# Token mixers as stepped generators between the halves of large weight products

## The chip, the cores and the metric

The kernel runs on one core of a Trainium2 chip: TensorE (PE) multiplies matrices into the eight banks of PSUM, VectorE (DVE), ScalarE (ACT) and GpSimd (POOL) do the elementwise work, and SyncE (SP) issues all the transfers of this kernel in one queue. Each engine takes its instructions in the order in which the program lists them. The metric is device time of one execution in microseconds (us), median of several runs.

## The reference

Two layers of a decoder trunk run over 280 columns: 16 meta tokens, 256 prompt tokens and one token of each of 8 samples. Per layer:

```
proj = x @ w_in                       # 16,400 columns: Mamba-2, HGRN2, retention, gates
y_m = mamba_branch(z, xbc, dt, ...)   # conv, silu, SSD recurrence, 4 groups of 4 heads
y_h = hgrn_branch(q, f, i, g, ...)    # gated linear recurrence, 8 heads of 128 x 128
y_r = retention_branch(q, k, v, g, ..)# 4 heads, keys 256, values 512, rotary
mixed = g_m*(y_m @ w_br_m) + g_h*(y_h @ w_br_h) + g_r*(y_r @ w_br_r)
x = LN1(alpha*x + mixed @ w_out)
x = LN2(alpha*x + SwiGLU(x))          # width 2816
```

The prompt runs through each recurrence in chunk form (scores of token pairs, weighted by decays, times values); each sample updates a stored state by one token. All new states are outputs. Everything is float32.

## The kernel before, in words

The stream stands transposed: a tile is 128 channels by 280 tokens. A **block** is 128 output columns of a weight matrix: `wblock` loads it into `raw`, ACT copies its high part to `wh`, DVE subtracts to get the rest in `wl`, and `project` (called by `in_block` and `br_block`) makes 24 **large products** of it on PE into a `pp` bank, three for each of 8 slices of the contraction. Layer 1 skips the 16 meta columns where nobody reads them, so many of its products have 264 columns.

The **mixers** are the three recurrences. They are many **small products** (128x128 transposes, products with 16 to 512 columns, many of them only 32 output columns wide) with elementwise work between them, in `mx`, `vb` and `po` banks.

- `hgrn_mix` handles a pair of heads. It builds eight levels of decayed operands (`level`: POOL subtracts the reference from the upper half and the lower half of each block, ACT takes the exponential, DVE multiplies by q and k, or POOL where the half length is 64 or more), and `diag` multiplies each level, 18 products of 32 or 24 columns. Masked sums (`pr`, `pt`, `scz`) then go into the output products. `hgrn_samples` updates eight samples' states.
- `mamba_group` and `mamba_samples` do the same for a group of four SSD heads; `ret_mix` and `ret_samples` for a retention head. `ret_samples` is already a generator: `tick`, called after each block, runs one step of it.
- `behind` makes the first of a group of small products wait for the last of all their operands.

In program order a whole stage of blocks stands first and the mixers that its predecessor fed come after it: stage p is `hgrn_proj(p + 1)`, six blocks, and four blocks of gates, then `hgrn_mix(p)`, `hgrn_samples(p)`, `mamba(p + 1)`. A scheduler at build time orders each engine's instructions by program order among those it holds to be ready, so small products fall between large ones where it expects a large one to wait. Weight splits get ahead by `boost` places of the program order (`BOOST`).

The stages that the text speaks of, per layer, with the blocks that bound them: A, B and C (10 blocks each: the projections of head pairs 1, 2 and 3 with their gates), D (8 blocks, retention head 0), E (8 blocks, retention head 1), then the tail (retention heads 2 and 3, the Mamba branch product, the three merge gates and the HGRN branch product; 56 blocks).

Of the kernel before, what the change touches and what calls it, by code (L numbers as in the profile page):

```python
# [8 lines left out]
F32 = mybir.dt.float32  # L9
# [6 lines left out]
P = 128  # L16
# [4 lines left out]
BUFS = {"px": 8, "py": 22, "pa": 10, "pm": 9, "tt": 3, "tm": 4, "ps": 2, "pb": 1, "vh": 4}  # L21
# [3 lines left out]
BOOST = (0, 10, 60)  # L25

RATE = 1
# [59 lines left out]
def body(ctx: ExitStack, tc: tile.TileContext, a: dict):  # L87
# [65 lines left out]

    def mm(out, lhsT, rhs, start, stop):
        return TE.matmul(out, lhsT, rhs, start=start, stop=stop, skip_group_check=True)  # L155
# [39 lines left out]
    def project(ps, w, rhs_hi, rhs_lo, nk, first=True, last=True):  # L195
        late[0] -= 1
        n = 1 if late[0] < 0 else nk
        for k0 in range(0, nk, n):
            for part in range(2):
                for k in range(k0, min(k0 + n, nk)):  # L200
                    hi, lo = (x[:, k, :] for x in w)
                    if part == 0:
                        mm(ps, hi, rhs_hi(k), first and k == 0, False)
                        mm(ps, lo, rhs_hi(k), False, False)
                    else:
                        mm(ps, hi, rhs_lo(k), False, last and k == nk - 1)
# [9 lines left out]
    later = []  # L216
    credit = [0.0]

    def tick(n=RATE):
        credit[0] = credit[0] + n if later else 0.0  # L220
        while later and credit[0] >= 1:
            credit[0] -= 1
            if next(later[0], 0) == 0:
                later.pop(0)
# [253 lines left out]
    flip = [0]  # L478

    def diag_of(parts):  # L480

        t = qd[flip[0] % 2]
        flip[0] += 1
# [48 lines left out]
    def ret_mix(l, h, proj):  # L532
# [21 lines left out]
        sub(end[64:96, 256:272], sc[0:32, 416:432], f32(end[0:32, 256:272]))  # L554

        vhl = flat("vh", dt=F32R)
        vt = []
        for t0, n in TOK:
            ps = mxt()
            for j in range(4):  # L560
                TE.transpose(ps[:n, 128 * j:128 * j + 128], blk(vch, j)[:, t0:t0 + n], ident)
# [4 lines left out]
            else:  # L566
# [3 lines left out]
                vt.append((hi, lo))  # L570
        kt = [pair("pm", 256, F32R), pair("pm", 256, F32R)]
        for tb, (t0, n) in enumerate(TOK):
            ps = mxt()
            for i in range(2):
                TE.transpose(ps[:n, 128 * i:128 * i + 128], k[:, i, t0:t0 + n], ident)
            kd = kdc[:n, tb, h:h + 1]
            hi, lo = (end[0:32, 0:256], end[64:96, 0:256]) if n < P else (kt[0][:, tb, :], kt[1][:, tb, :])
            V.tensor_scalar(hi, ps[:n, 0:256], kd, None, ALU.mult)
            stt(lo, ps[:n, 0:256], kd, f32(hi), ALU.mult, ALU.subtract)
        V.tensor_copy(end[32:64, 0:256], f32(end[0:32, 0:256]))  # L580

        y = pairs("py", 2)
        for j in range(4):
# [8 lines left out]
            copy(blk(y, j)[:, 0:TP], ps[:, 0:TP])  # L592

        def final(after=None):
            for i in range(2):
                so = flat("pm")
                ps = mxt()
                ks = slice(128 * i, 128 * i + 128)
                for tb in range(2):
                    (vh, vl), (kh, kl) = vt[tb], (x[:, tb, ks] for x in kt)  # L600
                    ins = mm(ps, kh, vh, tb == 0, False)
                    if after is not None and tb == 0:
                        nosync(raw(ins), raw(after))
                    mm(ps, kh, vl, False, False)
                    mm(ps, kl, vh, False, False)
                mm(ps, end[0:96, ks], vhl[0:96, :], False, True)
                copy(so, ps)
                store(out=a["ret_p"][l, h, i], in_=so)

        if h < 3:  # L610
            final()
        return y, vhl, columns(q, k), final

    def ret_norm(y):
        sq = pairs("pm", 2)
        for j in range(2):
            S.activation(sq[j][:, :, 0:TP], y[j][:, :, 0:TP], AF.Square)
        add(sq[0][:, :, 0:TP], sq[0][:, :, 0:TP], sq[1][:, :, 0:TP])
        add(sq[0][:, 0, 0:TP], sq[0][:, 0, 0:TP], sq[0][:, 1, 0:TP])
        st = mxt()  # L620
# [6 lines left out]
    def ret_samples(l, h, y, vhl, qk):  # L627
        gam = 1.0 - 2.0 ** (-5.0 - h)
        t = diag_of([qk[:, i, :] for i in range(2)])
        acc = po.tile([P, 512], F32, tag="po", name="po")  # L630
# [21 lines left out]
        os_ = flat("ps")  # L652
        copy(os_[:, 0:256], acc[:, 0:256])
# [132 lines left out]
    def mamba_tok(dd):  # L786
# [3 lines left out]
        for tb, (t0, m) in enumerate(TOK):  # L790
            TE.transpose(ps[:m, 128 * tb:128 * tb + 128], tk[:, t0:t0 + m], ident)
# [9 lines left out]
    def mamba_group(l, g, tok, dab, x, bc):  # L801
        Bc, Cc = blk(bc, g), blk(bc, 4 + g)
        btok = flat("pm", 384).rearrange("p (j t) -> p j t", j=3)
        xd = [pair("pm", 256), pair("pm", 256)]
        xdt = [xd[0][:, 0, :], xd[0][:, 1, :], xd[1][:, 0, :]]
        xt = [pair("pm", 256), pair("pm", 256)]
        xtl = [xt[0][:, 0, :], xt[0][:, 1, :], xt[1][:, 0, :]]
# [6 lines left out]
        copy(cb[0:32, 0:16], ps[0:32, 0:16])  # L814
        ps = mxt()
        for tb, (t0, n) in enumerate(TOK):
            TE.transpose(ps[:n, 128 * tb:128 * tb + 128], Bc[:, t0:t0 + n], ident)
        copy(btok[:, 0:2, :], ps[:, 0:256].rearrange("p (j t) -> p j t", j=2))
        S.activation(btok[0:32, 2, :], ps[0:32, 256:384], AF.Copy, scale=tmask[0:32, :])
        for tb, (t0, n) in enumerate(TOK):  # L820
            ps = mxt()
            for i in range(2):
                TE.transpose(ps[:n, 128 * i:128 * i + 128], x[g][:, i, t0:t0 + n], ident)
            mul(xdt[tb][:n, :].rearrange("p (h q) -> p h q", q=64), ps[:n, 0:256].rearrange("p (h q) -> p h q", q=64),
                tok[:n, tb, 4 * g:4 * g + 4].unsqueeze(2).to_broadcast([n, 4, 64]))
            mul(xtl[tb][:n, :].rearrange("p (h q) -> p h q", q=64), xdt[tb][:n, :].rearrange("p (h q) -> p h q", q=64),
                tok[:n, tb, 64 + 4 * g:64 + 4 * g + 4].unsqueeze(2).to_broadcast([n, 4, 64]))
        rows = dr.tile([NS, 256], F32, tag="rows", name="rows")
        store(out=rows, in_=xdt[2][24:32, :])

        ps = mxt()
        for tb, (t0, n) in enumerate(TOK):
            mm(ps[:, 0:256], btok[:n, tb, :], xtl[tb][:n, :], tb == 0, tb == 2)
        so = flat("pm", 256)
        copy(so, ps[:, 0:256])
        store(out=a["ssm_p"][l, g], in_=so)
        for i in range(2):
            b = 2 * g + i
            es = []
            for hh in range(2):  # L840
                h = 2 * b + hh
                pe = mxt()
                mm(pe[:, :SW], selh[:, h:h + 1].to_broadcast([P, P]), r32(cumhl), True, False)
                mm(pe[:, :MW], identb, negb, False, True)
                e = flat("pm", SW)
                act(e[:, 160:SW], pe[:, 160:SW], AF.Exp, bias=tok[:, 0, 32 + h:33 + h])
                act(e[:, 16:160], pe[:, 16:160], AF.Exp, bias=tok[:, 1, 32 + h:33 + h])
                act(e[0:32, 0:16], pe[0:32, 0:16], AF.Exp, bias=tok[0:32, 2, 32 + h:33 + h])
                mul(e[:, 16:SW], e[:, 16:SW], cb[:, 16:SW])
                up = mul(e[0:32, 0:16], e[0:32, 0:16], cb[0:32, 0:16])  # L850
                es.append(e)

            py = mxt()
            for tb, (t0, n, c0, c1) in enumerate(((0, P, 160, SW), (128, P, 16, 160), (256, 32, 0, 16))):
                for hh, e in enumerate(es):
                    hs = slice(64 * (2 * i + hh), 64 * (2 * i + hh) + 64)
                    ins = mm(py[64 * hh:64 * hh + 64, t0:TP], xdt[tb][:n, hs], e[:n, c0:c1], tb == 0, tb == 2)
                    if tb == hh == 0:
                        behind(ins, up)
            yv = x[g][:, i, 0:TP]  # L860
            stt(yv, yv, pcol(("dskip", l), b), py[:, 0:TP], ALU.mult, ALU.add)
        return rows

    def mamba_samples(l, g, dab, vhl, x, bc):
        Bc, Cc = blk(bc, g), blk(bc, 4 + g)
        t = diag_of([Cc[:, TP:T]])
        acc = po.tile([P, 512], F32, tag="po", name="po")
        for c in range(2):
            st = state(a["s_ssm"][l, g, c], "p (b q) -> p b q", b=4)
            s4 = st.rearrange("p b (h q) -> p b h q", q=64)  # L870
            mul(s4, s4, dab[:, 4 * c:4 * c + 4, 4 * g:4 * g + 4].unsqueeze(3).to_broadcast([P, 4, 4, 64]), G)
            for bb in range(2):
                vb = everywhere(vhl, 2 * c + bb)
                for b2 in range(2):
                    b = 4 * c + 2 * bb + b2
                    up = stt(st[:, b % 4, :], vb[:, 256 * b2:256 * b2 + 256], Bc[:, TP + b:TP + b + 1],
                             st[:, b % 4, :], ALU.mult, ALU.add)
# [568 lines left out]
```

## Time and profile before

| | us |
|---|---|
| median of 3 runs | 1934.88 (1929.5 to 1938.77) |
| the profiled execution, its own time | 1943.87 |
| its span, first to last instruction | 1941.8 |
| PE busy in the span | 1855.2 (96%) |
| DVE busy | 1360.4 (70%) |
| ACT busy | 1066.7 (55%) |
| POOL busy | 467.6 (24%) |
| mean granted clock of TensorE | 0.978 of full |

The profile is of one execution, 9 us above the median of the plain runs. Matmuls are pipelined, so a busy PE can still be a PE at half its clock or one that changes its tile shape between products.

### The profile page before, as it was taken

Reading aid. Unit: us, or ns where it says so; the run is one execution under the profiler, and the core shown is the slowest. Engines: PE = TensorE matmul, PEld = TensorE weight load, DVE = VectorE, ACT = ScalarE, POOL = GpSimd, SP = SyncE. Lnnn points to the kernel's source line nnn. Section 1 sums busy time; section 2 is a strip of 40 time slices with the busy share of each in tenths; the row PEclk is TensorE's granted clock in tenths of the full one; section 3 lists DMA queues with packets and bytes.
Section 4 is the critical chain, followed back from the end, with each engine's and each line's share of the span. In section 5 each row is a group of like instructions: output and inputs, shape, how many; then the busy total and the mean of one; then the engine's idle time right before and its main releaser. Section 6 shows DMA issues by size and latency. Waiting matters only on the chain.

```text
span 1941.8 us, 39091 instructions
## 1 busy us (share of the span) xinstructions
PE 1855.2 (96%) x15746; PEld 1718.3 (88%) x15746; DVE 1360.4 (70%) x2129; ACT 1066.7 (55%) x1826; POOL 467.6 (24%) x526
## 2 busy tenths in 40 slices
PE   8989999999999999999999999999999999999997
PEld 7978787888888999999989787878888889989997
DVE  7787877867656675655468899987767557666654
ACT  6666655545554544544356776755556546454443
POOL 2025535511011023000120255544110010230002
PEclk9989998999999999999999999999999999999999
DMA  5544564557678555455545446655766875545553
GB/s 198 182 152 170 191 211 162 200 209 256 224 283 299 196 174 165 140 174 173 164 137 173 163 165 204 209 201 184 249 231 248 293 263 182 184 144 183 181 176 102
DMA packets 115125, 378.44 MB, mean 195 GB/s; under 512 B 13120, under 2 KB 18688, under 8 KB 114944
## 3 DMA queue, kind: packets, MB, share of 16 engines
q1 hardware_dynamic: 114944, 375.94, 57.5%
q8 instruction: 124, 2.03, 0.4%
q14 instruction: 57, 0.47, 0.1%
HBM read 317.61 MB, written 58.28 MB: 194 GB/s over the span
## 4 chain that ended last, share of the span: by engine, by line
PE 77%; DVE 10%; DMA 5%; ACT 4%; issue 2%; POOL 1%; SPq 0%; DVEq 0%; ACTq 0%; POOLq 0%
PE pp L155 63%; PE mx L155 9%; DVE pm L140 3%; PE po L155 3%; DMA st<-s_ret 2%; DVE wl L140 2%; PE vb L155 1%; DVE pa L140 1%; ACT wh L137 1%; DMA ret_s<-st 1%; DVE py L140 1%; DVE st L152 1%; POOL hpt L140 1%; ACT pm L137 1%; POOL pm L140 1%
## 5 line engine op out<-in xcount | busy, mean ns | idle before, releaser
L155 PE MATMUL pp<-px,wh 128*128 128x280 f32 (+1 forms) x5504 | 1100.9, 295 | 17.9 <-DVE px L285 7.8
L155 PEld LDWEIGHTS pp<-px,wh 128*128 128x128 f32 x5504 | 889.4, 192 | 32.5 <-issue 13.5
L140 DVE TENSOR_TENSOR wl<-raw,wh 128x1024 fp32r<-128x1024 f32 (+1 forms) x472 | 608.6, 1292 | 307.2 <-ACT wh L137 302.9
L155 PE MATMUL pp<-px,wl 128*128 128x280 f32 (+1 forms) x2752 | 808.1, 294 | 0.5 <-DVE wl L140 0.5
L137 ACT ACTIVATE wh<-raw 128x1024 fp32r<-128x1024 f32 (+1 forms) x472 | 493.9, 1048 | 330.6 <-PE pp L155 207.0
L155 PEld LDWEIGHTS pp<-px,wl 128*128 128x128 f32 x2752 | 528.1, 192 | 6.2 <-issue 2.9
L155 PE MATMUL pp<-py,wh 128*128 128x280 f32 (+1 forms) x1984 | 381.6, 289 | 1.2 <-ACT py L137 0.8
L155 PEld LDWEIGHTS pp<-py,wh 128*128 128x128 f32 x1984 | 313.6, 188 | 3.9 <-issue 1.6
L155 PE MATMUL pp<-py,wl 128*128 128x280 f32 (+1 forms) x992 | 285.9, 288 | 1.5 <-DVE wl L140 1.5
L155 PEld LDWEIGHTS pp<-py,wl 128*128 128x128 f32 x992 | 186.7, 188 | 2.9 <-DVE wl L140 2.0
L155 PE MATMUL mx<-pm 128*32 128x16 f32 (+11 forms) x1968 | 144.8, 238 | 22.9 <-DVE pm L140 16.6
L155 PEld LDWEIGHTS mx<-pm 128*32 128x32 f32 (+4 forms) x1968 | 107.0, 136 | 55.4 <-issue 15.4
L140 POOL TENSOR_TENSOR pa<-pa 128x280 f32<-128x280 f32 (+3 forms) x56 | 76.8, 1381 | 310.3 <-DVE pa L140 249.7
L140 POOL TENSOR_TENSOR pm<-pm 128x272 f32<-128x272 f32 (+2 forms) x104 | 106.1, 1050 | 109.3 <-ACT pm L137 92.2
L152 DVE SCALAR_TENSOR_TENSOR st<-vb,qks,st 128x512 f32<-128x512 f32 x128 | 90.6, 745 | 53.0 <-PE vb L155 21.4
L140 DVE TENSOR_TENSOR pa<-pa,pp 128x280 f32<-128x280 f32 (+1 forms) x152 | 66.2, 435 | 47.2 <-PE pp L155 35.0
L130 ACT ACTIVATE pa<-pp 128x280 f32<-128x280 f32 (+1 forms) x124 | 48.4, 391 | 92.2 <-PE pp L155 92.2
L643 ACT ACTIVATE st<-st 128x1024 f32<-128x1024 f32 x64 | 67.7, 1057 | 56.3 <-DMA st<-s_ret 39.1
L140 POOL TENSOR_TENSOR pa<-px 128x560 f32<-128x560 f32 (+1 forms) x16 | 25.4, 1589 | 275.2 <-DVE py L140 275.0
L155 PE MATMUL po<-st,qd 128*32 128x256 f32 (+1 forms) x896 | 71.6, 369 | 1.7 <-DVE st L152 1.7
L137 ACT ACTIVATE pa<-pp 128x280 f32<-128x280 f32 (+1 forms) x80 | 31.7, 396 | 71.1 <-PE pp L155 70.8
L137 ACT ACTIVATE pm<-mx 128x256 f32<-128x256 f32 (+5 forms) x120 | 47.6, 412 | 40.9 <-PE mx L155 29.0
(233 smaller groups left out, 1800.2 us busy)
## 6 DMA issues: line engine op xcount, KB each, us to landing
raw<-w_in SPq DMA_DIRECT2D x256, 512.0 KB, 3.4
raw<-w_ffn_in SPq DMA_DIRECT2D x88, 512.0 KB, 3.2
st<-s_ret SPq DMA_DIRECT2D x64, 512.0 KB, 5.2
ret_s<-st SPq DMA_DIRECT2D x64, 512.0 KB, 3.7
vh<-rows SPq DMA_DIRECT2D x64, 256.0 KB, 4.6
raw<-w_br_r SPq DMA_DIRECT2D x32, 512.0 KB, 3.3
raw<-w_ffn_out SPq DMA_DIRECT2D x32, 512.0 KB, 3.9
st<-s_ssm SPq DMA_DIRECT2D x16, 512.0 KB, 4.8
```

Of the source, the lines that this page charges most:

```text
L130: ins = S.activation(out, in_, func, **kw)
L137: return S.activation(out, in_, AF.Copy)
L140: return e.tensor_tensor(out, x, y, op)
L152: return V.scalar_tensor_tensor(out, x, s, y, op0, op1)
L155: return TE.matmul(out, lhsT, rhs, start=start, stop=stop, skip_group_check=True)
L643: S.activation(st, st, AF.Copy, scale=gam)
```

## The change

`hgrn_mix`, `hgrn_samples` and `hgrn_final` become one generator, `hgrn`; the Mamba functions become `mamba`; `ret_mix` becomes a generator too. A step between two `yield`s holds one group of small products and the elementwise work of operands that a later step multiplies. `begin` puts a generator into `plan` with the number of its steps and of the half blocks they are spread over, and `tick` now runs after each half of a block (after slice 3 of 8 and at its end) and advances every generator in `plan` by its share. `put` ties each small product behind the last large product that the program has listed, without a semaphore. The mixers of pair p now run during the blocks of pair p + 1, one stage sooner for HGRN; `finish` runs what is left of them at the end of a stage.

Level subtraction becomes one DVE instruction over the whole block, an absolute value on ACT, and an exponential of the negative. `behind` goes. Turned tails (the transposed last 32 tokens) go to half of one fixed bank (`ends`), sample sums to its other half (`sums`), so the `mx` bank of the tails' scores is free again. Weight splits of the mixers' and later stages get ahead by 100 places. `pm` has 12 buffers in place of 9, and smaller tiles get 7 of their own (`pq`).

```diff
-BUFS = {"px": 8, "py": 22, "pa": 10, "pm": 9, "tt": 3, "tm": 4, "ps": 2, "pb": 1, "vh": 4}
+BUFS = {"px": 8, "py": 22, "pa": 10, "pm": 12, "pq": 7, "tt": 3, "tm": 4, "ps": 2, "pb": 1, "vh": 4}
-BOOST = (0, 10, 60)
-RATE = 1
+BOOST = (0, 100, 100)
+NM, NH, NR, NSR = 16, 17, 15, 12
...
+    place = [None]
+    def large(out, lhsT, rhs, start, stop):
+        place[0] = raw(TE.matmul(out, lhsT, rhs, start=start, stop=stop, skip_group_check=True))
+    def put(ins):
+        if place[0] is not None:
+            nosync(raw(ins), place[0])
+        return ins
...
+            if n == 1 and k0 == nk // 2 - 1:
+                tick()
...
+    plan = []
+    def begin(gen, steps, halves, credit=0.0):
+        plan.append([gen, steps / halves, credit])
+        return plan[-1]
+    def tick():
+        for s in list(plan):
+            s[1:] = s[1], s[2] + s[1]
+            while s[2] >= 1:
+                s[2] -= 1
+                if next(s[0], 0) == 0:
+                    plan.remove(s)
+                    break
...
+    both = po.tile([P, 512], F32, tag="po", name="po")
+    sums, ends = both[:, 0:256], both[:, 256:512]
...
-                sub(eu, cu, ref, G)
-                sub(el, ref, cl, G)
-                act(e[:, :, 0:n], e[:, :, 0:n], AF.Exp)
+                c4, e4 = (x[:, :, 0:n].rearrange("p i (b h) -> p i b h", h=2 * h) for x in (cum, e))
+                sub(e4, c4, c4[:, :, :, h - 1:h].to_broadcast([P, 2, nb, 2 * h]))
+                S.activation(e[:, :, 0:n], e[:, :, 0:n], AF.Abs)
+                act(e[:, :, 0:n], e[:, :, 0:n], AF.Exp, scale=-1.0)
...
+        e1 = level(1)
+        yield 1
+        diag(0, k, q)
+        yield 1
...
+        diag(1, k, e0)
+        e3 = level(3)
+        yield 1
+        diag(2, e1, e1)
+        e4 = level(4)
+        yield 1
...
-        hp = [hgrn_gate(l, 0, tiles)]
...
+        for p in range(4):
+            begin(hgrn(l, p, hp, hg, oh), NH, 19)
+            begin(mamba(l, p, td, dd, xm, bc, z, ym), NM + 2 * (p == 0), 19)
             if p < 3:
-                hp.append(hgrn_proj(l, p + 1))
-                z.append(smooth_pair(l, "py", True))
-                hg.append(smooth_pair(l, "py", False))
+                hp = hgrn_proj(l, p + 1)
+                z, hg = smooth_pair(l, "py", True), smooth_pair(l, "py", False)
+                finish()
...
-            smp = hgrn_mix(l, p, hp[p])
-            hgrn_samples(l, p, *smp)
...
-                mamba(p + 1)
...
+        rps = [rp]
+        begin(retention(), 4 * NR, 64)
...
+                    begin(samples(), 4 * NSR, 112)
...
-    nc = _bacc.Bacc("TRN2", target_bir_lowering=False, num_devices=1, dynamic_dma_scratch_size=8192)
+    nc = _bacc.Bacc("TRN2", target_bir_lowering=False, num_devices=1, dynamic_dma_scratch_size=2048)
```

## Rows read from the trace of the kernel before

**Rows 1.** The page's busy times by engine, and TensorE's granted clock in 40 slices.

```profile
PE 1855.2 (96%) x15746; PEld 1718.3 (88%) x15746; DVE 1360.4 (70%) x2129; ACT 1066.7 (55%) x1826; POOL 467.6 (24%) x526
...
PEclk9989998999999999999999999999999999999999
```

**Rows 2.** Busy time by stretch, layer 0: stages A to E, then the tail.

```profile
core 0: us, PE busy (x) PEld busy (x) DVE busy (x) ACT busy (x) POOL busy (x), PEclk, DMA share, GB/s
106.40:160.00 53.60, 47.59 (x395) 41.73 (x394) 43.56 (x71) 30.98 (x68) 25.98 (x19) 0.90 0.52 171
160.00:223.30 63.30, 59.64 (x637) 51.09 (x634) 50.73 (x97) 40.77 (x94) 26.10 (x29) 0.95 0.54 188
223.30:287.60 64.30, 59.86 (x637) 51.17 (x634) 50.55 (x98) 40.82 (x94) 29.58 (x33) 0.95 0.57 194
287.60:348.20 60.60, 54.24 (x587) 45.88 (x585) 46.35 (x100) 33.43 (x79) 33.51 (x37) 0.92 0.51 175
348.20:394.10 45.90, 42.36 (x457) 38.24 (x454) 34.88 (x65) 25.40 (x50) 21.92 (x31) 0.96 0.55 187
394.10:648.40 254.30, 250.20 (x1919) 222.25 (x1917) 162.83 (x231) 135.17 (x209) 29.01 (x28) 1.00 0.74 255
```

**Rows 3.** The same view, layer 1: stages A to E, then the tail.

```profile
1079.60:1129.70 50.10, 45.33 (x396) 39.93 (x394) 45.94 (x69) 32.62 (x70) 22.81 (x16) 0.93 0.50 170
1129.70:1191.30 61.60, 57.12 (x635) 49.26 (x633) 55.11 (x103) 43.49 (x98) 27.12 (x33) 0.97 0.55 189
1191.30:1253.00 61.70, 57.28 (x637) 49.16 (x635) 55.67 (x103) 43.14 (x98) 37.29 (x36) 0.97 0.58 200
1253.00:1311.60 58.60, 53.10 (x589) 44.79 (x586) 49.97 (x103) 34.26 (x81) 32.34 (x37) 0.94 0.58 198
1311.60:1357.60 46.00, 42.78 (x455) 39.21 (x454) 35.60 (x65) 25.21 (x50) 22.76 (x32) 0.93 0.57 188
1357.60:1606.50 248.90, 244.41 (x1920) 215.61 (x1918) 163.83 (x231) 134.63 (x209) 26.98 (x29) 1.00 0.73 255
```

**Rows 4.** Timeline, TensorE, stage B, layer 0: start, length; pp are large products.

```profile
164.96 0.42 PE L155 MATMUL pp<-px,wh 128*128 128x280 f32 x2
...
165.35 0.42 PE L155 MATMUL pp<-px,wh 128*128 128x280 f32 x2
...
166.78 0.42 PE L155 MATMUL pp<-px,wh 128*128 128x280 f32 x2
167.12 0.52 PE L155 MATMUL mx<-pm 128*32 128x16 f32 x36
167.57 0.40 PE L155 MATMUL pp<-px,wl 128*128 128x280 f32 x1
...
172.61 2.96 PE L155 MATMUL mx<-pm 128*128 128x128 f32 x24
176.63 0.80 PE L155 MATMUL mx<-pm 128*128 128x128 f32 x2 [1.05 <-POOL pm L140]
...
181.05 0.67 PE L155 MATMUL pp<-px,wh 128*128 128x280 f32 x2
...
181.75 0.67 PE L155 MATMUL pp<-px,wh 128*128 128x280 f32 x2
```

**Rows 5.** TensorE's longest waits in stages A to E of layer 1.

```profile
engine line waited for: us in total, times, longest us
PE mx L155 <- DVE pm L140: 9.1, 9, 2.4
PE mx L972 <- ACT pm L137: 9.0, 3, 3.8
```

**Rows 6.** DVE by groups, stage B, layer 1: count, busy, mean ns, idle before.

```profile
L140 DVE TENSOR_TENSOR pm<-pm,pa 128x544 f32<-128x544 f32 x1 | 0.7, 726 | 0.4 <-ACT pm L130 0.4
```

**Rows 7.** Groups of POOL's instructions in stage B of layer 1.

```profile
L140 POOL TENSOR_TENSOR pm<-pm 128x256 f32<-128x256 f32 x6 | 6.5, 1108 | 4.5 <-PE mx L155 4.5
L140 POOL TENSOR_TENSOR pm<-pm 128x272 f32<-128x272 f32 x5 | 6.3, 1275 | 0.0
```

**Rows 8.** Groups of ACT's instructions in stage B of layer 1.

```profile
L130 ACT ACTIVATE pm<-pm 128x544 f32<-128x544 f32 x3 | 1.8, 640 | 0.0
```

More of the change, by code (lines that the diff above doesn't have):

```diff
@@ L213, in body, with finish @@
     lead = 0
[L216 to L224, printed above, removed]
+    plan = []
[10 more added lines that the diff above has]
+                    break
+    def finish(*some):
+        some = list(some or plan)
+        while some:
+            for s in list(some):
+                if s not in plan or next(s[0], 0) == 0:
+                    some.remove(s)
+                    if s in plan:
+                        plan.remove(s)
     def in_block(l, c0=0):
@@ L592, in ret_mix @@
             copy(blk(y, j)[:, 0:TP], ps[:, 0:TP])
[L594 to L617, printed above, removed]
+            if j % 2:
+                sq.append(pair("pm"))
+                S.activation(sq[-1][:, :, 0:TP], y[j // 2][:, :, 0:TP], AF.Square)
+            yield 1
         add(sq[0][:, :, 0:TP], sq[0][:, :, 0:TP], sq[1][:, :, 0:TP])
         add(sq[0][:, 0, 0:TP], sq[0][:, 0, 0:TP], sq[0][:, 1, 0:TP])
+        yield 1
+        for i in range(2):
+            if h < 3:
+                final(i)
+            yield 1
         st = mxt()
@@ L628, in ret_samples @@
         gam = 1.0 - 2.0 ** (-5.0 - h)
-        t = diag_of([qk[:, i, :] for i in range(2)])
-        acc = po.tile([P, 512], F32, tag="po", name="po")
+        t = diag_of([qk[:, i, :] for i in range(2)], h % 2)
+        acc = sums
         def products(b):
@@ L814, in mamba_group, with weighted @@
         copy(cb[0:32, 0:16], ps[0:32, 0:16])
+        yield 1
+        def weighted(out, v, w, n):
+            mul(out.rearrange("p (h q) -> p h q", q=64), v.rearrange("p (h q) -> p h q", q=64),
+                w.unsqueeze(2).to_broadcast([n, 4, 64]))
+        xd, xt = pair("pm", 256), pair("pm", 256)
+        xde, xte = flat("pq", 256), flat("pq", 256)
+        ps = sums
+        for i in range(2):
+            turn(ps[:32, 128 * i:128 * i + 128], x[g][:, i, TAIL:T])
+        weighted(xde[:32], ps[:32, 0:256], tok[:32, 2, heads], 32)
@@ new lines, in mamba @@
+        weighted(xte[:32], xde[:32], tok[:32, 2, 64 + 4 * g:68 + 4 * g], 32)
+        rows = dr.tile([NS, 256], F32, tag="rows", name="rows")
+        store(out=rows, in_=xde[24:32, :])
+        yield 1
+        ps = mxt()
+        for tb in range(2):
+            for i in range(2):
+                turn(ps[:, 256 * tb + 128 * i:256 * tb + 128 * i + 128], x[g][:, i, 128 * tb:128 * tb + 128])
+        for tb in range(2):
+            weighted(xd[:, tb, :], ps[:, 256 * tb:256 * tb + 256], tok[:, tb, heads], P)
+            weighted(xt[:, tb, :], xd[:, tb, :], tok[:, tb, 64 + 4 * g:68 + 4 * g], P)
@@ L815, in mamba_group @@
+        yield 1
+        btok, be = flat("pq", 256), flat("pq", P)
         ps = mxt()
         for tb, (t0, n) in enumerate(TOK):
[L817 to L827, printed above, removed]
@@ L831, in mamba_group @@
+        scores(4 * g)
+        yield 1
         ps = mxt()
-        for tb, (t0, n) in enumerate(TOK):
-            mm(ps[:, 0:256], btok[:n, tb, :], xtl[tb][:n, :], tb == 0, tb == 2)
-        so = flat("pm", 256)
+        for tb in range(2):
+            mm(ps[:, 0:256], btok[:, 128 * tb:128 * tb + 128], xt[:, tb, :], tb == 0, False)
+        mm(ps[:, 0:256], be[:32], xte[:32], False, True)
+        so = flat("pq", 256)
         copy(so, ps[:, 0:256])
         store(out=a["ssm_p"][l, g], in_=so)
[L837 to L868, printed above, removed]
+        yield 1
+        scores(4 * g + 1)
+        yield 1
+        t = diag_of([Cc[:, TP:T]], 0)
+        acc = sums
+        def states(c):
             st = state(a["s_ssm"][l, g, c], "p (b q) -> p b q", b=4)
             s4 = st.rearrange("p b (h q) -> p b h q", q=64)
-            mul(s4, s4, dab[:, 4 * c:4 * c + 4, 4 * g:4 * g + 4].unsqueeze(3).to_broadcast([P, 4, 4, 64]), G)
+            mul(s4, s4, dab[:, 4 * c:4 * c + 4, heads].unsqueeze(3).to_broadcast([P, 4, 4, 64]), G)
@@ L886, in mamba_samples @@
+        scores(4 * g + 2)
+        yield 1
+        outputs(0)
+        yield 1
+        scores(4 * g + 3)
+        yield 1
+        read(st, 0)
+        st = states(1)
+        yield 1
+        outputs(1)
+        yield 1
+        read(st, 1)
+        os_ = flat("ps", 256)
+        copy(os_, acc)
+        yield 1
         for i in range(2):
-            mm(ps[:, 8 * i:8 * i + 8], os_[:, 128 * i:128 * i + 128], sumsel, True, True)
+            mm(acc[:, 8 * i:8 * i + 8], os_[:, 128 * i:128 * i + 128], sumsel, True, True)
@@ L904, in mamba_final @@
             stt(t[:, i, c], t[:, i, c], pcol(("mnw", l), 2 * g + i), rs, ALU.mult, ALU.mult)
-        return split(t)
+        ym.append(split(t))
     def hgrn_blocks(l, tiles):
@@ L1037, in hgrn_mix @@
         mul(kt[:, :, 0:TP], kt[:, :, 0:TP], k[:, :, 0:TP])
-        E = [level(LEVELS[x], 256) for x in range(4, 8)]
+        yield 1
+        diag(4, e3, e3)
         late_q = wk.tile([P, 2, 16], F32, tag="hlq", bufs=2, name="hlq")
@@ L1264, in body @@
         res.norm(("ln1_g", l), ("ln1_b", l))
-        smp[3](res.last)
+        for i in range(2):
+            final(i, res.last)
         hid = ([], [])
```

377 lines of the change are left out of this document (215 added, 162 removed).

## The prediction

> **What bounds the kernel now.** I read the page first: PE is busy nearly throughout, and its granted clock is below full in a few slices only [rows 1]. Since a share over the whole span hides the stages, I then asked for the busy times of the stages in which the mixers run. PE stands idle there for the length less its busy time: in A to E 6.0 + 3.7 + 4.4 + 6.4 + 3.5 = 24.0 us in layer 0 [rows 2] and 4.8 + 4.5 + 4.4 + 5.5 + 3.2 = 22.4 us in layer 1 [rows 3]; in the tails 4.1 and 4.5 us. The granted clock is 0.90 to 0.97 in A to E and 1.00 in the tails. [...] All that PE could gain is then 55.0 us of waits and 32.3 us of clock, 87 us.
>
> The timeline shows where both come from. Large products follow each other by 0.13 us (three in 0.39 us [rows 4]). Then a run of 24 small ones starts at 172.61, a wait for POOL of 1.05 us follows, and no large product stands between; afterwards three large ones take 0.70 us in place of 0.39, half the clock. The waits of A to E are for DVE's and ACT's results, up to 3.8 us at once [rows 5].
>
> The second thing to see is DVE. In stages B and C of layer 1 it works 55.1 to 55.7 of 61.6 us [rows 3], in layer 0 50.7 of 63.3 [rows 2]. PE at full clock and without waits would need 57.1 - 1.8 = 55.3 us in layer 1's B. Two engines have the same floor there.
>
> **The change part by part.** *Large and small products*: their numbers stay. Counting the breaks in PE's timeline gives 79 visits to small products in A to E of each layer, one per half block already, and some 140 in a whole layer. After it I count from the steps some 145. A visit costs little of its own: 36 products of 16 columns between two large ones delay the second by 167.57 - 166.91 - 0.13 = 0.53 us, nearly all their own 0.52 [rows 4]. I cost the new visits at nothing; if each of 20 more per pair cost half a visit, that is a rival below.
>
> *Spreading*: a stretch like 172.61 to 178 cannot come up where each half block, 12 large products and some 1.5 us, has one step of each generator behind it. I expect the clock to stay up in A to E, and PE's floors to be what it is busy now less the clock's share: in layer 0 A 42.2, B 56.5, C 56.6, D 49.4, E 40.5 us [rows 2], in layer 1 41.8, 55.3, 55.4, 49.6, 39.6 [rows 3].
>
> *HGRN one stage sooner*: it leaves E and enters A. Its work on PE is B less A, 14.3 and 13.5 us; on DVE 50.7 - 43.6 = 7.2 and 55.1 - 45.9 = 9.2. So A becomes a stage like B, and E needs 26.2 and 26.1 us of PE, 27.7 and 26.4 of DVE. In sum nothing, but the retention steps begin on a freer E.
>
> *Level subtraction*: six per pair go from two POOL instructions each to one on DVE. DVE takes 6 x 0.70 us (a two-input instruction of 544 elements takes 0.726 us, 512 elements are 6% less) = 4.2 us a pair [rows 6]. POOL loses some 13 us a pair [rows 7]. Instructions of DVE and POOL that run side by side slow each other, by how much in sum no row says: nothing given back is one bound, all 4.2 us the other; I take half, so DVE gains 2 us of work a pair. ACT takes six more of 0.62 to 0.64 us [rows 8], at most 3.8 us a pair; it is busy 43.5 of 61.6 us [rows 3] and this hides in its 18 us. Without that cover it would cost 8 x 3.8 = 30 us.
>
> *Queues*: POOL's multiplications of states and of the coarse levels come sooner, with 13 us of subtraction gone ahead of them. SP gets the mixers' loads, broadcasts and stores between the weight loads of the same stage, one stage earlier for HGRN; a store that waits for its data holds the next weight load behind it. The transfers fill 0.50 to 0.58 of the engines in A to E [rows 2, 3], and three raw and four split buffers stand ahead of PE, over 20 us at 6 us a block. I take nothing. *Banks, buffers, dropped semaphores, scratch*: a bank less is held over the levels; sums and tails share a bank and may wait for each other. Nothing either way, inside the allowance below. *Splits 100 places ahead*: no work, but mixer instructions on DVE stand behind them; also in the allowance.
>
> *The sum.* Each stage takes its larger floor and an allowance for waits. Today B of layer 0 stands 6.8 us above its floor and B of layer 1 6.3; with operands made steps ahead I allow 2.5 us (E, nearly empty, 1.5). Layer 0: A, B, C 59.0 each, D 51.9, E 29.2: 258.1 against 287.7, -29.6. Layer 1, where DVE's floor is the larger one (57.1, 57.1, 57.7, 52.0, 26.4): 59.6 + 59.6 + 60.2 + 54.5 + 27.9 = 261.8 against 278.0, -16.2. The tails have 8.6 us of waits; their steps were spread before, so I take 2. Together -48 us. The profiled execution, 1943.87, becomes 1896; the median of the plain runs stands 9 us lower, and 1934.9 - 48 = 1887.
>
> **The rivals.** *A wait at each visit (slower).* PE is in order: a small product that waits holds the second half of its block too. Visits number some 290 in both layers and today's waits 55 us, 0.19 us each. With all the clock regained the change loses once a visit waits 87 / 290 = 0.30 us; at 0.40 us it costs 116 - 87 = 29 us more: 1964. For it: DVE already at 0.9 in layer 1, given more work and the splits in front of the mixers', single waits of up to 3.8 us. Against: those waits come now from operands asked for at once, and the new steps make them one or more half blocks, 3 us, ahead.
>
> *DVE, or tile shapes, eat the gain (no change).* If POOL gives nothing back and each stage stays as far above its floor as now, 6.5 us, eight stages lose 4 us each and layer 1 another 2 each: 48 - 32 - 8 leaves -8 us, 1927. The other road to the same place is more openings of narrow tile shapes: 20 more visits a pair, the two generators' groups apart, at half of 0.53 us are 5.3 us a pair, 42 us for eight: 1929. Against the second: the groups themselves stay whole, and by the steps as written a pair has 56 changes of tile shape where I count 57 now. [...]
>
> *The order on PE stays as it was (no change).* The scheduler places instructions by what it holds ready, and small products stood between large ones before. Then 8 x 2 us on DVE count at most in layer 1's four pairs: 1935 to 1943.
>
> *All of it (faster still).* No allowance (-23 us), the tails' waits gone (-6.6), POOL giving back all (-6): 1851.
>
> **How the numbers follow.** About 0.5%, 10 us, is what a measurement of this kernel can tell from no change. The forecast case, 1870 to 1905, gets 0.46; a weaker one, with an allowance between 2.5 and 6 us, 1905 to 1925, gets 0.14; below 1870 0.13; no change 0.13; the waits 0.14. So faster 0.73, same 0.13, slower 0.14. The range runs from the full gain, 1852, to 1942, where the slower case begins; the forecast's own is 1870 to 1905.
>
> **What would show it.** Right: granted clock of 0.99 or more in A to D; A as long as B and C, 58 to 61 us; E at 28 to 32; PE's idle time in A to E at half or less of 46 us; POOL's busy time down by about 100 us and DVE's up by no more than 20. Wrong: large products that wait for wl, or small ones for DVE, at most visits; DVE busy for a whole stage with PE idle by 5 us; the clock still falling inside A to E, which would mean that steps bunch up as before.

## The result and the profile after

The kernel after the change takes 1910.39 us (median of 4 runs, 1903.8 to 1915.73), the kernel before 1934.73 beside it: a ratio of 0.9874 [0.9835, 0.9913], 24.3 us less. The forecast was 48 us less, 1887 us, in a range of 1870 to 1905. The profiled execution went from 1943.87 to 1915.73 us, 28.1 us less, and the stages below are compared in these two.

The page of the kernel after, busy times and granted clock, answers to [rows 1]:

```profile
PE 1838.5 (96%) x15746; PEld 1710.0 (89%) x15746; DVE 1351.5 (71%) x2177; ACT 1078.4 (56%) x1838; POOL 392.5 (21%) x430
...
PEclk9998999999999999999999989999999999999999
```

POOL lost 75.1 us. DVE, which took over 48 level subtractions, did not gain but lost 8.9 us. The stages answer to [rows 2, 3]: A to E and the tail of layer 0, then of layer 1:

```profile
core 0: us, PE busy (x) PEld busy (x) DVE busy (x) ACT busy (x) POOL busy (x), PEclk, DMA share, GB/s
105.80:176.60 70.80, 61.47 (x641) 52.30 (x639) 59.61 (x124) 47.50 (x107) 28.36 (x24) 0.93 0.51 171
176.60:238.20 61.60, 57.29 (x636) 49.33 (x634) 53.89 (x106) 43.41 (x97) 22.76 (x22) 0.99 0.63 208
238.20:300.20 62.00, 58.11 (x635) 50.34 (x634) 52.44 (x105) 43.29 (x97) 20.32 (x21) 0.97 0.59 201
300.20:348.00 47.80, 47.80 (x559) 41.17 (x557) 41.43 (x93) 32.21 (x72) 15.95 (x20) 0.98 0.59 191
348.00:387.60 39.60, 39.33 (x298) 36.83 (x295) 27.58 (x49) 22.80 (x40) 8.54 (x10) 1.00 0.50 168
387.60:626.10 238.50, 236.90 (x1860) 213.78 (x1859) 155.15 (x212) 125.17 (x188) 30.01 (x27) 1.00 0.76 270
1057.50:1128.60 71.10, 60.40 (x635) 51.17 (x634) 60.69 (x120) 47.27 (x105) 26.45 (x23) 0.90 0.47 155
1128.60:1189.20 60.60, 57.87 (x636) 49.47 (x635) 55.16 (x110) 45.07 (x101) 20.57 (x22) 0.97 0.57 196
1189.20:1248.40 59.20, 56.46 (x636) 49.09 (x635) 55.36 (x109) 44.36 (x99) 20.02 (x23) 0.97 0.61 211
1248.40:1300.40 52.00, 49.53 (x566) 42.03 (x564) 47.11 (x95) 34.28 (x76) 22.74 (x24) 0.97 0.62 210
1300.40:1340.20 39.80, 38.79 (x299) 36.31 (x296) 27.78 (x50) 22.80 (x40) 8.01 (x11) 1.00 0.51 174
1340.20:1576.00 235.80, 232.12 (x1860) 207.12 (x1859) 154.34 (x212) 124.95 (x188) 30.25 (x28) 1.00 0.76 265
```

HGRN's products did move: A has some 640 products where it had 395, E 298 where it had 457. From A to the tail's end layer 0 takes 520.3 us in place of 542.0, layer 1 518.5 in place of 526.9, together 30.1 us less; 2 us of it are lost elsewhere. Of the 30.1, PE's idle time (length less busy) gives 12.3: it was 55.0 with the tails, and is now 17.8 + 19.6 in A to E and 5.3 in the tails, 42.7. The other 17.8 are PE's busy time; the mean clocks account, as an estimate, for up to 11.6 of it: length times (1 - PEclk), added up over A to E, gives 8.4 + 12.3 = 20.7 us here and 18.4 + 13.9 = 32.3 us in [rows 2, 3].

Against the forecast, stage by stage: B and C measure 61.6, 62.0, 60.6 and 59.2 us for 59.0 to 60.2; D 47.8 and 52.0 for 51.9 and 54.5; E and tail together 278.1 and 275.6 for 282.5 and 275.8. Only A is far off: 70.8 for 59.0 and 71.1 for 59.6. These two, +11.8 and +11.5 us, are more than the 19.7 us by which the profiled execution misses its own forecast, 1896; the other stages together give a little back. What PE waits for in A of layer 1:

```profile
engine line waited for: us in total, times, longest us
PE pp L158 <- ACT pa L998: 4.6, 1, 4.6
PE mx L167 <- POOL pm L140: 4.5, 2, 4.2
PE mx L167 <- DVE pm L140: 1.4, 2, 1.0
```

The timeline of the kernel after around the 4.2 us in the second line, POOL first, then DVE, then PE (start, length, the wait before it in brackets):

```profile
1088.81 0.19 POOL L525 COPY qks<-pa 128x16 f32<-128x16 f32 x1
1091.62 11.18 POOL L140 TENSOR_TENSOR hpt<-hpt 24x16 f32<-24x16 f32 x4 [2.63 <-DVE hpt L140]
1102.87 0.20 POOL L1231 COPY scz<-hpt 24x32 f32<-24x32 f32 x1
1103.03 2.76 POOL L140 TENSOR_TENSOR pm<-pm,pa 128x256 f32<-128x256 f32 x4
...
1093.98 1.21 DVE L140 TENSOR_TENSOR wl<-raw,wh 128x1024 fp32r<-128x1024 f32 x1
...
1100.22 1.65 DVE L152 SCALAR_TENSOR_TENSOR st<-vh,qks,st 128x128 f32<-128x128 f32 x6
1101.79 0.59 DVE L152 SCALAR_TENSOR_TENSOR pq<-pq,hdc,mx 128x128 f32<-128x128 f32 x2
...
1106.99 0.28 DVE L1213 COPY scz<-mx 64x128 f32<-64x128 f32 x1 [4.21 <-ACT scz L137]
...
1104.48 1.14 PE L167 MATMUL mx<-pm 128*64 128x64 f32 x8 [4.22 <-POOL pm L140]
```

POOL has four additions of 24x16 to do, the tail's sums over the levels (`gather(pt[0:24], 16, lev, G)`). They take 11.2 us, and nearly all of it is the first one, as the same view shows in two windows:

```profile
1091.62 10.32 POOL L140 TENSOR_TENSOR hpt<-hpt 24x16 f32<-24x16 f32 x1 [2.63 <-DVE hpt L140]
...
1102.02 0.79 POOL L140 TENSOR_TENSOR hpt<-hpt 24x16 f32<-24x16 f32 x3
```

DVE works without a gap all the while: 28 instructions start in these 10 us, each before the one ahead of it has ended and each with both of its tensor inputs in SBUF. The last of them (st<-vh,qks,st) ends at 1101.86. The next (pq<-pq,hdc,mx) takes one input from PSUM, and POOL's addition ends at 1101.94. The three that are left take 0.21 us each. By these times the first addition was not slowed evenly, it was held up until DVE's row was over. Two other long ones of the kernel after, 3.88 us in A of layer 0 and 3.64 us in B of layer 1, also end 0.08 us after the last of such a row. The kernel before has the same effect, less of it: the first addition takes 3.15 to 3.94 us in four of its eight pairs, and in the other four, stage B of layer 1 among them, the four together take 0.9 to 1.0 us.

The coarse multiplications (pm<-pm,pa) stand behind the additions, and PE's small products behind those. No large product goes ahead of the small ones: the last before the wait starts at 1099.78, the next at 1106.30. DVE then runs dry for 4.2 us, and TensorE's granted clock, full from 1100 to 1103, averages 0.69 from 1103 to 1106.

### The profile page after: what moved, and what is told of

Its sections match the earlier page's. It is cut to its first block, busy times and chain, and to the rows that moved or that the text cites. A ratio compares the mean times of both kernels' runs of the same rounds, so it can differ in the third digit from the quotient of the medians.

```text
span 1913.9 us, 38948 instructions
## 1 busy us (share of the span) xinstructions
PE 1838.5 (96%) x15746; PEld 1710.0 (89%) x15746; DVE 1351.5 (71%) x2177; ACT 1078.4 (56%) x1838; POOL 392.5 (21%) x430
## 4 chain that ended last, share of the span: by engine, by line
PE 76%; DVE 10%; DMA 5%; ACT 4%; issue 3%; POOL 2%; SPq 0%; DVEq 0%; ACTq 0%; POOLq 0%
PE pp L158 63%; PE mx L167 9%; DVE wl L140 2%; DMA st<-s_ret 2%; PE po L167 2%; DVE pm L140 2%; PE vb L167 1%; ACT wh L137 1%; DVE pa L140 1%; POOL hpt L140 1%; DMA ret_s<-st 1%; DVE st L152 1%; PE mx L170 1%; DVE py L152 1%; DVE py L140 1%
## 5 line engine op out<-in xcount | busy, mean ns | idle before, releaser
L158 PE MATMUL pp<-px,wh 128*128 128x280 f32 (+1 forms) x5504 | 1122.9, 295 | 20.6 <-DVE px L317 7.8
L158 PEld LDWEIGHTS pp<-px,wh 128*128 128x128 f32 x5504 | 893.9, 191 | 40.0 <-issue 15.7
L140 DVE TENSOR_TENSOR wl<-raw,wh 128x1024 fp32r<-128x1024 f32 (+1 forms) x472 | 594.2, 1261 | 337.2 <-ACT wh L137 335.8
L687 ACT ACTIVATE st<-st 128x1024 f32<-128x1024 f32 x64 | 67.8, 1059 | 103.4 <-DMA st<-s_ret 83.7
L167 PE MATMUL mx<-pm 128*32 128x16 f32 (+8 forms) x1728 | 117.2, 232 | 9.1 <-POOL pm L140 7.0
L167 PEld LDWEIGHTS mx<-pm 128*32 128x32 f32 (+2 forms) x1728 | 88.1, 132 | 30.8 <-POOL pm L140 7.5
L140 DVE TENSOR_TENSOR pm<-pm 128x64 f32<-128x64 f32 (+7 forms) x176 | 85.7, 509 | 24.4 <-ACT pm L654 17.9
L130 ACT ACTIVATE pm<-pm 128x544 f32<-128x544 f32 (+4 forms) x112 | 58.0, 540 | 12.2 <-DVE pm L152 12.1
L130 ACT ACTIVATE pa<-pp 128x280 f32<-128x280 f32 (+1 forms) x124 | 47.3, 382 | 25.4 <-PE pp L158 25.3
L167 PE MATMUL po<-st,qd 128*32 128x256 f32 x640 | 55.8, 397 | 3.6 <-DVE st L152 3.4
```

The lines of the kernel that those rows point to most:

```text
L130: ins = S.activation(out, in_, func, **kw)
L140: return e.tensor_tensor(out, x, y, op)
L158: place[0] = raw(TE.matmul(out, lhsT, rhs, start=start, stop=stop, skip_group_check=True))
L167: return put(TE.matmul(out, lhsT, rhs, start=start, stop=stop, skip_group_check=True))
L687: S.activation(st, st, AF.Copy, scale=gam)
```

## The experiments

All were timed beside the kernel before, which took 1937.39, 1937.44 or 1938.18 us; the ratios are to it, and the stages of each run are read from one profiled execution. The theories that they are to tell apart: 1, short POOL instructions starve beside a dense DVE in A; 2, DVE's work itself is the bound; 3, the waits stand at a stage's edges, in its first steps or in the norm's product at its end; 4, the new order and the move of the level subtraction pay only together.

**tail_adds_dve**: the four additions a pair on DVE.

```diff
-            gather(pt[0:24], 16, lev, G)
+            gather(pt[0:24], 16, lev, V)
```

> The four additions of 24x16 elements per head pair that gather the tail's masked sums (gather of pt) go from POOL to DVE, nothing else. Theory 1, POOL starves: in stage A of layer 1 of the changed kernel these four take 11.2 us (about 1.0 us at their shortest), the coarse multiplications and PE's wait of 4.2 us come behind them, and the clock falls; without them on POOL, A of layer 1 shortens by 6 to 10 us, A of layer 0 by 3 to 6, B to D by 1 each: the changed kernel's 1910 becomes 1892 to 1900. Theory 2, DVE's work is the bound: eight pairs get 0.6 us more DVE work each, 1910 becomes 1912 to 1916. Theory 3, the first pair begins before its operands: A stays at 70 to 71 us, 1910.

1904.19 us (1899.17 to 1912.78), ratio 0.984 [0.9814, 0.9867]. Stage A of both layers by windows, columns as above:

```profile
104.80:171.10 66.30, 57.30 (x639) 49.11 (x638) 60.64 (x128) 47.03 (x107) 24.98 (x19) 1.00 0.52 174
1052.20:1116.80 64.60, 58.33 (x634) 49.38 (x633) 61.61 (x124) 46.98 (x105) 22.54 (x19) 0.95 0.51 169
```

A falls by 4.5 and 6.5 us, its clock rises from 0.93 and 0.90 to 1.00 and 0.95, and its waits for POOL's pm in layer 1 are gone, though DVE has more to do there. That speaks for theory 1 and against theory 2, though theory 1 had forecast 1892 to 1900. B, 63.0 and 63.3, takes 1.4 and 2.7 us more, and the interval of the whole overlaps that of the change, so this run alone shows no gain in time. What it shows is that the wait goes. How much of A's length hangs on the additions it does not show: in no_ties (below), which leaves them on POOL, the four take 2.5 us in A of layer 1 and A takes 64.7; in late_first they take 1.5 us there and A still takes 69.0.

**levels_pool** and **before_levels_dve**: the level subtraction on DVE and the rest of the change (order, steps, buffers, the splits' lead), each without the other. The first is the kernel after with the level subtraction on POOL again:

```diff
-                sub(e4, c4, c4[:, :, :, h - 1:h].to_broadcast([P, 2, nb, 2 * h]))
-                S.activation(e[:, :, 0:n], e[:, :, 0:n], AF.Abs)
-                act(e[:, :, 0:n], e[:, :, 0:n], AF.Exp, scale=-1.0)
+                ref = c4[:, :, :, h - 1:h].to_broadcast([P, 2, nb, h])
+                sub(eu, c4[:, :, :, h:2 * h], ref, G)
+                sub(el, ref, c4[:, :, :, 0:h], G)
+                act(e[:, :, 0:n], e[:, :, 0:n], AF.Exp)
```

> The level subtraction goes back to POOL, two instructions per level, and the absolute value on ACT goes, as in the kernel before; the rest stays changed. Theory 1, the two engines' shared traffic decides: POOL gets some 13 us a pair more, both engines hold each other up more, 1910 becomes 1915 to 1930. Theory 2, DVE's work is the bound: DVE loses 4.2 us a pair, the eight pair stages shorten by 1 to 3 us each, 1910 becomes 1890 to 1902.

The second is the kernel before with this edit turned round.

> The kernel before with one part of the change alone: the level subtraction as one DVE instruction, the absolute value on ACT; order, steps, buffers as before. Theory 1, taking POOL's work away is what pays, whatever the order: 1937 becomes 1905 to 1915, as fast as the changed kernel. Theory 4, the two parts need each other: with the old order PE still waits for clumped small products and the clock still falls, 1922 to 1935. Theory 2, DVE's work is the bound: 1940 to 1950.

| ratio to the kernel before | old order | new order |
|---|---|---|
| level subtraction on POOL | 1 | 1.0038 [1.0021, 1.0055], 1945.18 us |
| on DVE | 1.0070 [1.0052, 1.0089], 1951.97 us | 0.9874 [0.9835, 0.9913], 1910.39 us |

Each part alone makes the kernel slower, by 7.8 and 14.5 us; both together take 24.3 off, 46.6 more than the sum of the two. Theory 4 holds in this, that neither pays alone. Its range for before_levels_dve, 1922 to 1935, was too low; 1951.97 lies next to theory 2's, 1940 to 1950, but DVE has less to do there than in the kernel before (1356.3 us for 1360.4). levels_pool lies above both ranges given for it. The page's busy times of levels_pool, and PE's longest waits in it:

```profile
PE 1847.3 (95%) x15746; PEld 1714.1 (88%) x15746; DVE 1342.6 (69%) x2129; ACT 1052.9 (54%) x1790; POOL 468.1 (24%) x526
```

```profile
PE mx L167 <- ACT pm L130: 14.4, 6, 3.2
PE po L170 <- DVE pq L140: 10.4, 6, 3.2
```

DVE has 8.9 us less to do than in the kernel after, and the kernel takes 1.7% more, some 32 us: theory 2 falls. The exponentials (ACT's pm of L130) that end the six waits of the first line are Mamba's (pm<-mx,tok). In stage B of layer 1 they stand in ACT's order behind a level's exponential, and this waits for POOL's subtraction, which stands behind the four additions:

```profile
1173.67 2.22 POOL L140 TENSOR_TENSOR hpt<-hpt 24x16 f32<-24x16 f32 x4
...
1176.11 1.18 POOL L140 TENSOR_TENSOR pm<-pm 128x256 f32<-128x256 f32 x2
...
1177.33 0.63 ACT L130 ACTIVATE pm<-pm 128x512 f32<-128x512 f32 x1 [3.23 <-POOL pm L140]
1177.86 0.51 ACT L130 ACTIVATE pm<-mx,tok 128x144 f32<-128x144 f32 x2
...
1178.43 1.17 PE L167 MATMUL mx<-pm 128*64 128x272 f32 x2 [3.21 <-ACT pm L130]
```

So a late result on POOL holds up ACT, and through ACT's order another mixer's product. In before_levels_dve PE's longest waits are:

```profile
PE mx L155 <- POOL pm L140: 13.2, 8, 2.9
PE mx L155 <- DVE pm L140: 11.9, 12, 2.4
PE mx L972 <- ACT pm L137: 10.6, 7, 2.8
```

The wait for POOL's pm was 4.7 us in 4 over the whole kernel before. POOL has 89.5 us less to do (378.1 for 467.6), yet the first of its small additions in stage B of layer 1 takes 3.94 us, where it took 0.26, and ends 0.08 us after the last of a row of DVE's state updates (st<-vh,qks,st); coarse multiplications stand behind it. Why this comes up more often in the old order was not tried.

**no_finish** and **late_first**, for theory 3. In B and C of layer 0 PE's one wait is 4.3 and 3.9 us for the norm's product; no_finish leaves the early call to the pending steps away, so that what is left of them runs in the next stage. late_first begins the first pair's generators four half blocks later.

```diff
-                finish()
```

```diff
-            begin(hgrn(l, p, hp, hg, oh), NH, 19)
-            begin(mamba(l, p, td, dd, xm, bc, z, ym), NM + 2 * (p == 0), 19)
+            n, w = (15, 4) if p == 0 else (19, 0)
+            nm = NM + 2 * (p == 0)
+            begin(hgrn(l, p, hp, hg, oh), NH, n, -w * NH / n)
+            begin(mamba(l, p, td, dd, xm, bc, z, ym), nm, n, -w * nm / n)
```

> The forced run of what is left of the mixers at the end of stages A, B and C goes; the last step of each generator, the product with ones and the norm, then runs at the first half block of the next stage. Theory 1: PE waits 4.3 and 3.9 us at the ends of B and C of layer 0 for that step's operand, which DVE makes late; half a block more, 2 to 3 us, takes most of the two waits and the clock's fall after them away: 1910 becomes 1900 to 1905. Theory 2, DVE's work is the bound: the wait turns up at another product, 1908 to 1912.

> The generators of the first pair start four half blocks later in stage A and run at 15 half blocks in place of 19. Theory 3, the first pair begins before its operands are there: A shortens by 5 to 10 us in each layer, 1910 becomes 1892 to 1900. Theory 1, POOL starves behind a dense DVE: the same work in fewer half blocks, A stays or grows by up to 5 us, 1908 to 1920.

1913.35 us, 0.9878 [0.9858, 0.9899], and 1913.56 us, 0.9875 [0.9854, 0.9896]: no change against the kernel after. With late_first A takes 65.5 us in layer 0, 5.3 less, and 69.0 in layer 1, 2.1 less; B of layer 0 takes 64.5, 2.9 more. What A gains, other stages lose, and theory 3 falls for a stage's first steps.

no_finish does not test the other half, since the product that PE waits for did not move. It is the norm's product of Mamba, which a regular step and not the early call brings at the end of the stage; only HGRN's went over to the next one. It stands behind the same large product as in the kernel after, and waits 4.1 and 4.0 us in B and C for 4.3 and 3.9. What makes it late is the effect above turned round. In B of the kernel after, POOL's multiplication of Mamba's states starts first, and DVE's addition for the norm is held up beside it; three stretched DVE instructions (2.33, 2.45 and 2.14 us) lead up to the product:

```profile
233.73 2.20 POOL L140 TENSOR_TENSOR st<-st,dab 128x1024 f32<-128x1024 f32 x1 [1.37 <-DMA st<-s_ssm]
...
234.09 2.14 DVE L140 TENSOR_TENSOR pm<-pm 128x280 f32<-128x280 f32 x1
```

In states_act (below) the same addition meets no such multiplication:

```profile
229.43 0.44 DVE L140 TENSOR_TENSOR pm<-pm 128x280 f32<-128x280 f32 x1
```

**boost_back**: the splits' lead as before.

```diff
-BOOST = (0, 100, 100)
+BOOST = (0, 10, 60)
```

> The changed kernel with the weight splits' lead as before (10 places in the mixers' stages, 60 after them, in place of 100). If the lead delays the mixers' work on DVE (the allowance of the prediction), A to D shorten by 1 to 2 us each, 1910 becomes 1896 to 1904. If it is what keeps large products from waiting for their splits between the small ones, the large products wait for wl and 1910 becomes 1915 to 1930. If neither, 1908 to 1913.

1906.95 us, 0.9838 [0.9819, 0.9857]: 0.4% below the kernel after, with intervals that overlap, and outside all three ranges. A takes 66.4 and 67.9 us in place of 70.8 and 71.1, and large products wait 7.9 us for wl in place of 0.6. Part of PE's waiting is now for the weights.

**states_act**: HGRN's multiplication of the states, two POOL instructions a pair, as 16 small ones on ACT.

```diff
-            mul(st, st, fb, G)
+            for b in range(4):
+                for i in range(2):
+                    S.activation(st[:, b, i, :], st[:, b, i, :], AF.Copy, scale=fc[:, i, 4 * c + b:4 * c + b + 1])
```

> The changed kernel with HGRN's state multiplication taken from POOL (two instructions of 2.0 us a pair) to ACT (sixteen of some 0.3 us, 4.8 us a pair, with a column of scales each). Theory 1, POOL and DVE hold each other up: the DVE instructions that take 2.1 to 2.5 us beside it in place of 0.5 to 0.7 shrink, PE's waits at the ends of B and C of layer 0 (4.3 and 3.9 us) shrink with them: 1910 becomes 1894 to 1903. Rival: ACT, busy 43 to 47 us of 60 to 71 in A to C, becomes what PE waits for: 1910 to 1925.

1908.86 us, 0.9851 [0.9825, 0.9877], not to be told from the kernel after, and outside both ranges. What theory 1 said of the two norms' products came: their waits shrink to 0.5 and 0.3 us, and B and C of layer 0 take 5.9 us less together. A takes 63.5 and 68.0 us. But B and C of layer 1 take 12.1 us more, and the waits for POOL's pm grow from 7.0 to 15.7 us:

```profile
PE mx L167 <- POOL pm L140: 15.7, 9, 3.9
```

The 32 small additions, still on POOL, take 44.0 us in place of 32.0. Taking long work off POOL does not help its short work, as theory 1 has it.

**tail_and_states**: both edits.

> Both: the tail's four additions on DVE and HGRN's state multiplication on ACT; POOL keeps the Mamba states, the coarse multiplications and copies. Theory 1: the two gains add up, 1884 to 1896. Rival, DVE and ACT are full now: no faster than the better of the two alone, 1900 to 1912.

1896.23 us (1895.5 to 1899.81), 0.9787 [0.9767, 0.9807]: at the upper end of theory 1's range, the best version, below both kernels, with an interval below that of each edit alone. Its page, and its windows of A and B in both layers:

```profile
PE 1830.0 (97%) x15746; PEld 1703.6 (90%) x15746; DVE 1340.9 (71%) x2209; ACT 1112.3 (59%) x1966; POOL 354.9 (19%) x382
```

```profile
104.70:172.10 67.40, 60.52 (x640) 52.10 (x639) 55.11 (x126) 49.44 (x117) 18.30 (x17) 0.92 0.51 182
172.10:228.20 56.10, 55.14 (x630) 47.69 (x629) 49.52 (x107) 46.98 (x113) 13.69 (x14) 1.00 0.60 197
...
1046.80:1114.10 67.30, 58.84 (x635) 50.41 (x634) 59.09 (x125) 52.77 (x122) 20.03 (x17) 0.95 0.46 159
1114.10:1175.70 61.60, 59.06 (x640) 50.33 (x638) 54.64 (x117) 48.90 (x116) 17.50 (x16) 0.97 0.58 205
```

B of layer 0 falls below the forecast, to 56.1 us. A stays at 67, above the 66.3 and 64.6 of tail_adds_dve. There the next short work on POOL takes the additions' place, four multiplications of 0.72 us each at their shortest, one row of its timeline:

```profile
1082.55 9.33 POOL L140 TENSOR_TENSOR pm<-pm,pa 128x256 f32<-128x256 f32 x4 [5.97 <-ACT pm L130]
```

**three** is tail_and_states with the lead of boost_back; **four** is three with these multiplications on DVE as well (`e_ = V` for `e_ = G if h >= 64 else V`).

> The tail's additions on DVE, HGRN's state multiplication on ACT, and the splits' lead as before (10 and 60 places). Theory 1 with the lead as its own cost: the 7 us that the lead alone gave back add to the 41 us under the kernel before: 1885 to 1892. Rival, with POOL lighter the lead no longer costs anything: 1893 to 1900.

> As three, and the coarse levels' multiplications by q and k (four of 128x256 a pair, 1.2 us each on POOL, some 0.4 us on DVE) go to DVE too. Theory 1: PE's remaining waits for POOL go, 3 to 8 us under three. Theory 2, DVE's work is the bound by now: 1.7 us a pair more on DVE, 3 to 13 us over three.

1906.53 us, 0.9837 [0.982, 0.9854], and 1902.56 us, 0.9807 [0.9788, 0.9825]. The first lies above both of its ranges and is slower than tail_and_states, with intervals apart: the gain that boost_back seemed to have turns into a loss of some 10 us once POOL is lighter. PE's longest wait in three:

```profile
PE pp L158 <- DVE wl L140: 13.6, 11, 3.5
```

The lead of 100 is what feeds the large products then. four is 4 us under three, as theory 1 has it, but the intervals overlap. In four A of layer 0 comes down to 62.3 us, that of layer 1 stays at 67.8, and the waits for wl stay too (13.4 us in 8).

**block_ticks** and **no_ties** take the order itself: a step pair once a block in place of a step every half block; and no tie of a small product to the large one before it.

```diff
-            if n == 1 and k0 == nk // 2 - 1:
-                tick()
...
-        plan.append([gen, steps / halves, credit])
+        plan.append([gen, 2 * steps / halves, credit])
```

```diff
-            nosync(raw(ins), place[0])
+            pass
```

> The changed kernel with steps taken once a block, two at a time, in place of once a half block. Theory 4, the fine order itself pays: steps bunch, operands are a step less ahead, 1910 becomes 1920 to 1935. Rival, the order's grain does not matter while POOL and DVE are what PE waits for: 1905 to 1915.

> The changed kernel without the tie of each small product to the last large one listed before it. If the ties hold the written order, small products that the scheduler holds ready move ahead of large ones and bunch: 1915 to 1930. If the program order decides alone, 1908 to 1913.

block_ticks takes 1924.45 us, 0.9936 [0.9915, 0.9956], as theory 4 has it: against 0.9874 some 12 us, half of the gain, go with the half blocks. no_ties takes 1910.4 us, 0.9859 [0.9843, 0.9875]: the ties alone carry nothing that can be measured.

## Why the prediction was half right

**The step that failed** is "So A becomes a stage like B". I had priced A at PE's 56.5 and 55.3 us, raised to DVE's 57.1 in layer 1, with 2.5 us for waits. Measured, PE is busy 61.5 and 60.4 us in A and idle 9.3 and 10.7. Of the +11.8 and +11.5 us, 5.0 and 5.1 are busy time, which the clock of 0.93 and 0.90 alone could make (7% and 10% of 71 us), and the rest idle time. A is not like B in two ways that the profile of before could have told. DVE is busy 59.6 and 60.7 us in it, where I had added HGRN's share to A's and come to 52.7 and 57.1. I had taken B less A for that share, but in layer 0 of the kernel before twelve weight splits (18.5 us) fall in A and ten (16.5 us) in B, and A has preparations that B has not, so the difference was less than HGRN's work. And it is this dense DVE beside which POOL's chain starves, a term that my sum did not have: I had taken the slowing of one engine by the other as shared work, half of it given back, and not as a late result at the end of a chain. The size of this term stays open: without the additions on POOL A falls by 4.5 and 6.5 us, but other edits move A by as much. Open is also what holds A at 67 us in the best version. In layer 1 PE waits there 4.6 us for ACT to empty a PSUM bank (the row of L998, unchanged) and 3.0 for POOL, and neither was taken away by itself. In the first no work of POOL shows: in the kernel after ACT is busy almost without a gap, and three preparations stand between the two ACT instructions that empty the bank (1062.38 and 1064.93).

**Spreading** was right in direction, not in size. The clock stays at 0.97 to 0.99 in B to D where it was 0.92 to 0.97, not at 0.99 or more; by the estimate from lengths and mean clocks 20.7 of the 32.3 us are still lost, 12.1 of them in A. That estimate also gives the clock's share in the floors, and no run shows it, since none changes the clock alone; what the traces show is that three large products of [rows 4] take 0.39 us at a granted clock of 1.00 (160.0 to 172.6) and 0.70 us at 0.50 (181.0 to 182.5), 1.8 times as long. Idle time in A to E came to 37.4 us, not to half of 46. block_ticks bears the step out: the half block is worth some 12 us.

**Level subtraction.** The instruction costs what I said (0.73 us at 512 elements and 0.76 at 544, for 0.70). What POOL gives back was undersized: from levels_pool to the kernel after DVE rises by 8.9 us for some 36 us of added instructions (24 by 0.73 and 24 by 0.76), so three quarters come back, where I took half. POOL in turn fell by 75.1 us in place of about 100, since what stayed on it takes longer in sum; the means below mix held-up instructions with undisturbed ones:

```profile
L140 POOL TENSOR_TENSOR pm<-pm,pa 128x256 f32<-128x256 f32 x32 | 38.1, 1212 | 19.4 <-ACT pm L130 14.1 <-DVE pa L140 4.9
...
L140 POOL TENSOR_TENSOR hpt<-hpt 24x16 f32<-24x16 f32 x32 | 32.0, 998 | 17.2 <-DVE hpt L140 15.5
```

In the kernel before these were 777 and 617 ns in the mean; the two groups lose 26 us.

**E and the tail**: right in sum, wrong in place. E takes 39.6 and 39.8 us, not 28 to 32, because retention's steps move into it; the tails hold 59 and 60 products less and are 15.8 and 13.1 us shorter.

**Visits at nothing, splits 100 places ahead and shared banks in the allowance.** Visits to small products, counted in the traces, are 311 in both layers after the change, 276 before it and 229 in block_ticks. block_ticks has the fewest and is slower than the kernel after, so whatever a change of tile shape costs, finer steps give more here; the cost itself was not taken apart. The lead costs nothing that can be told from zero in the kernel after, and pays in the better one.

**The rivals.** "A wait at each visit" did not come: for 311 visits, where I forecast some 290, PE idles 42.7 us, 0.14 us each, where I had 0.19 from 55 us. "DVE eats the gain" forecast 1927, and its cause did not come: DVE has less work than before, and levels_pool shows that still less of it on DVE is slower. The case that came is the weaker one of the forecast, 1905 to 1925, to which I had given 0.14. It came in its number and not in its account: it spread a larger allowance over all stages, where one stage was far off and the others near their price.

## What to carry to other kernels

When work moves between DVE and POOL, price not only the busy time. Look for the longest row of DVE instructions with both inputs in SBUF that a short POOL instruction may have to sit out (28 of them here, 10.32 us for an addition of 0.21), and for the long POOL instruction that a short one of DVE may have to (2.14 us beside a multiplication of 2.20 us, 0.44 without it); then ask who waits for the result. A stage that inherits another's work is priced from its own rows on every engine, not from those of the stage that it comes to resemble. Try the parts of a change together before dropping one that loses alone: the finer order and the level subtraction on DVE each lost here, and won as a pair.

## What the runs showed that I had not expected

How long one short POOL instruction can be held up: an addition of 24x16 takes 0.21 us at its shortest and 10.32 us in A of layer 1, and PE's wait of 4.22 us shows that this is no mere mark of the profile. It goes both ways: POOL's addition started 0.15 us after a DVE instruction and took 10.32 us, DVE's addition for the norm started 0.36 us after a multiplication of POOL and took 2.14 us, where it took 0.44 without one in states_act. Nor had I expected that POOL got no turn between DVE's instructions. The longest of the 28 took 1.21 us, and the addition sat out all of them. In states_act one addition took 7.92 us and again ended 0.08 us after the last of such a row. Not every POOL instruction beside a dense DVE is caught: at 208.27 in the kernel after a multiplication of 128x256 took its 0.73 us, and the state update of DVE that started within 0.01 us of it took 0.90 in place of 0.33. Whether a gap put into DVE's row would let POOL in was not tried. Nor does less work on POOL help by itself: without the long multiplications of HGRN's states (states_act) the 32 additions took 44.0 us in sum, where the kernel after has 32.0.
